# Norm factors by token, a bonus product moved ahead, and a new table of step latencies in a two-layer hybrid decoder kernel

## The chip, the cores and the metric

The kernel runs on one core of one Trainium2 chip. The metric is the device time of one execution in microseconds (us). The core has TensorE (PE; PEld is its weight load), VectorE (DVE), ScalarE (ACT), GpSimd (POOL) and the queues that issue DMAs, SyncE's (SP) among them. Each engine runs its own instructions in the order in which they were emitted and waits on semaphores of the others.

## The reference, cut to what matters

Two layers over 288 tokens (a prompt of 256 and 8 samples of 4) of width 2048, in fp32. Layer 0 mixes by RWKV-7 beside SSD, layer 1 by a gated delta rule (GDN); each layer then has cross attention to a memory and a gated FFN with a short convolution.

```python
for l in range(DEPTH):
    hn = rmsnorm(h, P['norm_mix'][l])
    if l % 2 == 0:
        p_rw, p_ssd = jnp.split(hn @ P['w_in_ab'][i], [RW_PROJ], axis=-1)
        y_rw, sh, s_rw = rwkv7_mix(p_rw, ...)
        y_ssd, cb, s_ssd = ssd_mix(p_ssd, ...)
        mix = jnp.concatenate([y_rw, y_ssd], axis=-1) @ P['w_out_ab'][i]
    else:
        y_c, cb, s_gdn = gdn_mix(hn @ P['w_in_c'][i], ...)
        mix = y_c @ P['w_out_c'][i]
    h = h + mix
    h = h + cross_attn(rmsnorm(h, P['norm_xa'][l]), mem_k[l], mem_v[l], P['w_xq'][l], P['w_xo'][l])
    f, fb = conv_ffn(rmsnorm(h, P['norm_ffn'][l]), st_ffn[l], ...)
    h = h + f
y = rmsnorm(h, P['norm_final'])
```

`rmsnorm` multiplies each token's row by the reciprocal root of its mean square and by a gain. In RWKV each head adds to its output a bonus, the sum over its channels of r·k·rk times v. SSD's sample states follow h = h·decay + state increment. GDN's decay is g = -exp(A)·softplus(a + bias), and its chunks need a triangular solve, as RWKV's do.

## The kernel before, in words

Activations lie with features on the partitions and the 288 tokens along the row. A projection reads fp32 weights from HBM in blocks `raw` of 128x512, which ACT rounds to `wh` and DVE completes by the remainder `wl`; the activations are split likewise into `xH` and `xL`. Each 128x128 block of weights then takes three matmuls of 288 columns into `p_acc` (xH by wh, xL by wh, xH by wl). One such matmul is called a **W** below; there are some 19,900 of them, and in stretches with nothing else they start 0.133 us apart.

The normalization is not applied to the activations but to what a projection gives: `rB` holds each token's factor on all 128 partitions and multiplies `p_acc` when it leaves PSUM (`pad<-p_acc,rB`, `fu<-p_acc,rB`). Squares are summed into `sacc` as the residual `h` is written. `stats_end` then has one matmul of `sacc` with ones, which sums over partitions and spreads the sum over all of them, and a reciprocal root on DVE over 128x288 elements in 12 operations: one for the mean, two for a first guess and three Newton rounds of three (`nx`, `nt`, `rB` in the trace). It is called at six places: at the end of the memory part (for layer 0's mix), ahead of layer 0's cross attention and FFN, ahead of layer 1's mix, cross attention and FFN. The last normalization (`last_norm`) does it by token: three small matmuls a summand put each token's sum on a partition, GpSimd takes the power -1/2, and the factors come back onto all partitions by a diagonal `dg` and a matmul with ones.

In the mixed stages (RWKV with SSD, GDN, cross attention) the weights' matmuls serve as fill between the small steps of the heads. `flow()` is a planner: it holds several streams of jobs, each a generator that yields between steps. The first stream is the fill (projections), the others are prepare, invert, sample, chain and so on. It keeps a clock made of modelled matmul durations; step k of a job of kind `x` may not stand before `LAT[(x, k)]` us after the end of the step ahead of it (1.6 us where the table says nothing, 0 for the fill), and while no step is due it emits fill. What comes out is the order of TensorE's instructions, which is kept as emitted; the other engines are ordered by the tile scheduler.

Names that the steps touch. RWKV (kinds `rwp` prepare, `rwv` invert, `rwt` sample, `rwc` chain, `rwf`) takes 16 heads in 8 pairs: `rkk` is r·k·rk and its matmul with a block of ones `cst` goes to the only `p_row` bank; `AR,h` are the Gram matmuls into `p_ma`, masked into `Gm`; `at_r` and `a8t_r` start the inversion, whose steps are `a_r,a8t_r`, `sx_r,xt_r`, `xc_r,xt_r`, `lo_r,xt_r`, `mx_r,xt_r`, `xc_r,xt_r`, `ac_r,h`, `XTr,yc_r`. `finish` of a pair multiplies by the gate (`SG,gu`) and transposes y (`cst,yr`). SSD (`sdG`, `sdh`, `sd0`, `sdp`) has two groups of 8 sample states: `h<-i_sssd` is loaded, `h,Cx` reads it, `XDs,bs` makes the increment in a PSUM bank, and `hn` is the new state that is stored. GDN (`gdi` inputs, `gdp` prepare, `gdv` invert, `gds` and `gdt` sample, `gdc` chain, `gdf` last finish) takes 16 heads; its decay rows are made once at the start of the stage (`aa`, `sp`, `grows`, `d`), and the last step of its inversion is `X,Atg`, copied by ACT to `yh_g`, then `XTg,yh_g`.

Of the kernel before, what the change touches and what calls it, by code (L numbers as in the profile page):

```python
# [43 lines left out]
def _consts():  # L44
# [50 lines left out]
PV_HALF = POFF["g_mix"][0]  # L95
# [135 lines left out]
def pr(ap):  # L231
    return ap[:, :NP]
# [17 lines left out]
class K:  # L250
# [310 lines left out]
    def last_norm(self, sq):  # L561
# [3 lines left out]
        x = self.mp.tile([128, 3], F32, name="fx")  # L565
# [44 lines left out]
    def conv_silu(self, ps, hist, out_state, wcols, bias, out, out2=None):  # L610
# [170 lines left out]
    def rwkv(self):  # L781
# [53 lines left out]
        def prepare(j, o):  # L835
# [31 lines left out]
            self.stt(ta, ta, 1.0, kk, ADD, MUL)  # L867
            p = self.P("row")
# [36 lines left out]

            Gm = o.Gm = mp.tile([128, 4, 2, 128], F32, name="Gm", tag="Gm", bufs=2)
# [258 lines left out]
    def ssd(self):  # L1165
# [171 lines left out]
        def group(g, os):  # L1337
# [4 lines left out]
            for b in range(B):  # L1342
# [105 lines left out]
    def gdn(self):  # L1448
# [83 lines left out]
        def prepare(h, o):  # L1532
# [27 lines left out]
            for c in range(2):  # L1560
                self.stt(DEC[:, c, :], pb[:, c * 128:(c + 1) * 128], TOK[:, c, 32 + h:33 + h], self.c("negm"), SUB, ADD)
# [563 lines left out]
```

## Time and profile before

| | us |
|---|---|
| median of 3 runs (lowest, highest) | 3385.61 (3383.97, 3388.70) |
| the profiled execution | 3383.89 |
| its span in the trace | 3382.1 |
| memory part, 0 to 107 | 107 |
| layer 0 mix, 107 to 714; out-projection to 790; cross attention to 865 | 758 |
| layer 0 FFN, 865 to 1711 | 846 |
| layer 1 mix, 1711 to 2380; out-projection to 2444; cross attention to 2521 | 810 |
| layer 1 FFN and final norm, 2521 to 3382 | 861 |

The profile is one execution; its time is 1.8 us above the span of its trace and 1.7 us below the median. Stage limits are read off the first and last matmuls of each part, to a few us. TensorE is busy nearly all the time, so what counts is where it waits, and at which clock it runs.

### The profile page before, as it was taken

Reading aid. Unit: us, or ns where it says so; the run is one execution under the profiler, and the core shown is the slowest. Engines: PE = TensorE matmul, PEld = TensorE weight load, DVE = VectorE, ACT = ScalarE, POOL = GpSimd, SP = SyncE. Lnnn points to the kernel's source line nnn. Section 1 sums busy time; section 2 is a strip of 40 time slices with the busy share of each in tenths; the row PEclk is TensorE's granted clock in tenths of the full one; section 3 lists DMA queues with packets and bytes.
Section 4 is the critical chain, followed back from the end, with each engine's and each line's share of the span. In section 5 each row is a group of like instructions: output and inputs, shape, how many; then the busy total and the mean of one; then the engine's idle time right before and its main releaser. Section 6 shows DMA issues by size and latency. Waiting matters only on the chain.

```text
span 3382.1 us, 73169 instructions
## 1 busy us (share of the span) xinstructions
PE 3307.1 (98%) x27952; PEld 3130.2 (93%) x27952; DVE 2392.4 (71%) x5908; ACT 1799.3 (53%) x4435; POOL 86.6 (3%) x267
## 2 busy tenths in 40 slices
PE   9999999899999999999999999999999999999998
PEld 7888778789999999999988888888989999999998
DVE  7777777876766566556688888887776655665665
ACT  7655556545544444444556666666554444443444
POOL 0000000000000000000000000000000000000000
PEclk9999999899999999999999999999999999999999
DMA  8532233576555555555654444445755555555554
GB/s 259 191 99 93 89 101 124 163 235 213 170 165 164 167 163 168 163 165 166 186 154 142 143 147 144 141 145 170 234 181 162 163 166 165 165 166 163 167 165 144
DMA packets 194815, 547.20 MB, mean 162 GB/s; under 512 B 33824, under 2 KB 60064, under 8 KB 194464
## 3 DMA queue, kind: packets, MB, share of 16 engines
q1 hardware_dynamic: 194464, 542.52, 51.5%
q8 instruction: 220, 3.60, 0.4%
q14 instruction: 131, 1.07, 0.1%
HBM read 511.58 MB, written 30.86 MB: 160 GB/s over the span
## 4 chain that ended last, share of the span: by engine, by line
PE 89%; DVE 5%; issue 4%; ACT 1%; DMA 1%; POOL 0%; SPq 0%; DVEq 0%; ACTq 0%; POOLq 0%
PE p_acc L303 73%; PE p_ma L303 5%; PE p_mb L303 4%; PE p_row L303 3%; PE p_y L303 1%; DVE wl L315 1%; PE p_row L311 1%; DMA raw<-i_w_fi 1%; PE p_mb L311 0%; DVE hn L318 0%; ACT wh L328 0%; DVE h L315 0%; PE p_ma L311 0%; DVE cy L318 0%; DMA cache<-i_cv 0%
## 5 line engine op out<-in xcount | busy, mean ns | idle before, releaser
L303 PE MATMUL p_acc<-xH,wh 128*128 128x288 f32 x6464 | 1964.7, 304 | 6.8 <-ACT ost L328 2.9
L303 PE MATMUL p_acc<-xL,wh 128*128 128x288 f32 x6464 | 1912.7, 296 | 4.7 <-DVE xL L315 4.7
L303 PE MATMUL p_acc<-xH,wl 128*128 128x288 f32 x6464 | 1907.4, 295 | 3.8 <-DVE wl L315 3.7
L328 ACT ACTIVATE wh<-raw 128x512 fp32r<-128x512 f32 x1755 | 1100.0, 630 | 1229.7 <-PE p_acc L303 1091.4
L315 DVE TENSOR_TENSOR wl<-raw,wh 128x512 fp32r<-128x512 f32 x1755 | 1203.6, 689 | 621.9 <-ACT wh L328 592.1
L303 PEld LDWEIGHTS p_acc<-xH,wh 128*128 128x128 f32 x6464 | 1214.0, 188 | 36.7 <-issue 13.3
L303 PEld LDWEIGHTS p_acc<-xL,wh 128*128 128x128 f32 x6464 | 1217.1, 188 | 8.3 <-DVE xL L315 5.1
L303 PEld LDWEIGHTS p_acc<-xH,wl 128*128 128x128 f32 x6464 | 1219.0, 189 | 6.0 <-DVE wl L315 5.0
L315 DVE TENSOR_TENSOR pad<-p_acc,rB 128x256 f32<-128x256 f32 x348 | 93.0, 300 | 47.9 <-PE p_acc L303 47.4
L318 DVE SCALAR_TENSOR_TENSOR cy<-pad,pv,cy 128x312 f32<-128x312 f32 x180 | 95.8, 532 | 3.9 <-ACT cy L328 1.7
L318 DVE SCALAR_TENSOR_TENSOR fy<-pad,pv,fy 128x304 f32<-128x304 f32 x176 | 93.8, 533 | 3.1
L315 DVE TENSOR_TENSOR h<-p_acc,h 128x288 f32<-128x288 f32 x128 | 58.4, 456 | 43.6 <-PE p_acc L303 43.1
L592 POOL MEMSET pad<- 128x2 f32 (+2 forms) x174 | 17.5, 102 | 2458.4 <-DVE fy L318 1741.1
L315 DVE TENSOR_TENSOR fu<-p_acc,rB 128x288 f32<-128x288 f32 x88 | 40.2, 457 | 32.2 <-PE p_acc L303 32.2
L328 ACT ACTIVATE sq<-h 128x288 f32<-128x288 f32 x90 | 39.6, 440 | 26.5 <-DVE h L315 26.4
L315 DVE TENSOR_TENSOR sacc<-sacc,sq 128x288 f32<-128x288 f32 x104 | 47.1, 453 | 2.7 <-ACT sq L328 2.6
L315 DVE TENSOR_TENSOR fu<-fu,fy 128x256 f32<-128x256 f32 (+1 forms) x176 | 45.8, 302 | 2.2 <-ACT fy L328 2.2
L328 ACT ACTIVATE osc<-pad 128x3 f32<-128x3 f32 x120 | 22.9, 212 | 40.5 <-DVE pad L315 40.0
L328 ACT ACTIVATE xH<-h,pv 128x288 fp32r<-128x288 f32 x80 | 41.7, 521 | 0.0
L318 DVE SCALAR_TENSOR_TENSOR xL<-h,pv,xH 128x288 fp32r<-128x288 f32 x80 | 41.1, 514 | 0.5 <-ACT xH L328 0.3
L303 PE MATMUL p_acc<-oH,wh 128*128 128x288 f32 x128 | 38.2, 301 | 1.8 <-ACT wh L328 0.8
L315 DVE TENSOR_TENSOR xL<-fu,xH 128x288 fp32r<-128x288 f32 x88 | 39.8, 452 | 0.0
(672 smaller groups left out, 3220.7 us busy)
## 6 DMA issues: line engine op xcount, KB each, us to landing
raw<-i_w_fi SPq DMA_DIRECT2D x352, 512.0 KB, 3.6
raw<-i_w_fo SPq DMA_DIRECT2D x160, 512.0 KB, 3.6
raw<-i_w_c SPq DMA_DIRECT2D x128, 512.0 KB, 3.8
raw<-i_w_ab SPq DMA_DIRECT2D x92, 512.0 KB, 3.8
raw<-i_w_oab SPq DMA_DIRECT2D x32, 512.0 KB, 4.3
raw<-i_w_oc SPq DMA_DIRECT2D x32, 512.0 KB, 3.9
raw<-i_w_xkv SPq DMA_DIRECT2D x31, 512.0 KB, 4.6
raw<-i_w_xq SPq DMA_DIRECT2D x16, 512.0 KB, 4.7
```

Of the source, the lines that this page charges most:

```text
L303: i = self.pe.matmul(out, l, r, start=start, stop=stop)
L311: i = self.pe.transpose(out, a, self.c("ident", r)[:, r])
L315: (eng or self.v).tensor_tensor(out=out, in0=a, in1=b, op=op)
L318: self.v.scalar_tensor_tensor(out=out, in0=a, scalar=sc, in1=b, op0=o0, op1=o1)
L328: self.s.activation(out=out, in_=a, func=f, scale=scale)
L592: self.g.memset(p[:, 0:H], 0.0)
```

## The change

1. `stats_end` uses the by-token way of `last_norm` (now `token_norm`), with the single summand `sacc`; ACT copies the result to `rB`. At six places one large matmul and 12 DVE operations of 128x288 are replaced by three small matmuls, two small DVE operations, a GpSimd power, two DVE operations for `dg`, one large matmul and a copy.
2. RWKV: `rkk` is computed ahead of the first yield of its job, and its matmul and the product with v stand ahead of the Gram matmuls instead of behind them. `finish` yields between `SG,gu` and the transposes of y.
3. SSD: `hn` is made by two operations of 128x512 (decay times state, then plus the PSUM increment) instead of eight of 128x64.
4. GDN's start: the softplus is done with tokens on partitions, on 3x16 columns, and transposed back; SSD's softplus is in that layout already. All heads' decay matrices are made as separate jobs (`gde`) in a tile `DECS`, the factor `ed` goes into `KT_` and `KS` instead of into `u` and `US` (`ud`, `uds` fall away).
5. GDN's heads from 2 on (`EARLY`) take Silu from ACT instead of Tanh and a DVE product, so ACT's tables are loaded 8 times in the program where they were loaded 4 times.
6. `LAT`: `rwv` steps 1 to 8 go from 4.5, 1.6, 2.6, 1.6, ... to 2.7, 0.96, 1.56, 0.96, ...; `sdG` 2 from 0.4 to 2.2; `sdh` 4 from 1.6 to 0.3; `sd0` 0 from 1.6 to 0.96; `xas` 0 from 1 to 3.2; `xat` 4 from 0 to 1.1; `gdt` 6 from 1.6 to 2.1; `gdi` 0 (a fill job) from 0 to 2.4; `gdf` 0 from 1.6 to 5; `gde0` 0 is 18 and `gde` 0 is 1.6. All other entries are the same.
7. The columns of the packed vectors that are halved up front end ahead of `gw`; two small scaled copies `gwh` and `gnh` serve GDN's first two heads.

```diff
     def stats_end(self):
-        ps = self.P()
-        self.mm(ps[:, :N], self.ones, self.sacc)
-        x = self.gt("nx")
-        t = self.gt("nt")
         r = self.big.tile([128, N], F32, name="rB", tag="rB", bufs=2)
-        self.ts(x, ps[:, :N], 1.0 / D, MUL, EPS, ADD)
-        self.rsqrt(r, x, t)
+        self.act(r, self.token_norm([self.sacc]))
         self.rB = r
...
         for i, (r, t) in enumerate(parts):
-            self.mm(p[r, i:i + 1], self.sacc[:, t], self.ones[:, 0:1], stop=False)
-            self.mm(p[r, i:i + 1], sq[:, t], self.ones[:, 0:1], start=False)
+            for n, sq in enumerate(sums):
+                self.mm(p[r, i:i + 1], sq[:, t], self.ones[:, 0:1], start=n == 0, stop=n == len(sums) - 1)
...
             self.stt(ta, ta, 1.0, kk, ADD, MUL)
+            rkk = gt("rkk")
+            self.stt(rkk, r, self.pcol("rk", j), kp, MUL, MUL)
             p = self.P("row")
             yield 2
...
             yield 3
 
+            p = self.P("row")
+            self.mm(p[:, :N], bo64, rkk)
+            self.stt(self.h[:, j, :], p[:, :N], 64.0, v, MUL, MUL)
+
             Gm = o.Gm = mp.tile([128, 4, 2, 128], F32, name="Gm", tag="Gm", bufs=2)
...
-            rkk, BV = gt("rkk"), self.h[:, j, :]
-            self.stt(rkk, r, self.pcol("rk", j), kp, MUL, MUL)
-            p = self.P("row")
-            self.mm(p[:, :N], bo64, rkk)
-            self.stt(BV, p[:, :N], 64.0, v, MUL, MUL)
...
             self.mm(pg[:, :N], o.gu, SG)
+            yield
             p = self.P("mb")
...
                 hn = al("hn", [128, 512], "UV")
-                for h in range(8):
-                    x = slice(64 * h, 64 * h + 64)
-                    self.stt(hn[:, x], h0[:, x], q.CD[:, 8 * g + h, 1 + b:2 + b], ph[:, x], MUL, ADD)
+                self.tt(hn.rearrange("p (h x) -> p h x", x=64), h0.rearrange("p (h x) -> p h x", x=64),
+                        q.CD[:, 8 * g:8 * g + 8, 1 + b:2 + b].to_broadcast([128, 8, 64]), MUL)
+                self.tt(hn, hn, ph, ADD)
                 self.store(d["o_ssds"][b][:, gs], hn)
...
-        self.softplus(x, rg, lambda: gt("sp")[rg])
+
+        p = self.P()
+        self.transpose3(p, rows)
+        xt = mp.tile([128, 3, 48], F32, name="gtt")
...
+        self.softplus(xt[:, :, rg], None, lambda: gt("sp")[:, 0:48].rearrange("p (c x) -> p c x", c=3))
+        p = self.P()
...
         with self.ordered():
-            self.flow(fill, prep, inv, smp, chn)
+            self.flow(fill, dec, prep, inv, smp, chn)
```

How the order changes, at three places. Line numbers of the helpers are one higher in the changed program (L303 is L304, L315 is L316, L318 is L319).

The first place is RWKV's sixth pair of heads. On TensorE the rows of before stand so; between the two `AR,h` there are 12 W, which are left out:

```order
L303 MATMUL p_ma<-AR,h 128x128 x4
L303 MATMUL p_mb<-UV,Gm 64x64 x2
...
L303 MATMUL p_ma<-AR,h 128x128 x4
L303 MATMUL p_row<-rkk,cst 128x288
L303 MATMUL p_mb<-R,XTr 64x64 x2
L303 MATMUL p_acc<-xH,wh 128x288
```

And on DVE, where `rkk` is made in before, behind the masking of the two Gram products:

```order
L315 TENSOR_TENSOR Gm<-p_ma,cst 128x512
L322 TENSOR_SCALAR mu<-mu 32x2
L315 TENSOR_TENSOR Gm<-p_ma,cst 128x512
L315 TENSOR_TENSOR ys<-ys,mu 32x128
L315 TENSOR_TENSOR h<-Gm,rk_5406 64x4x64 x2
L318 SCALAR_TENSOR_TENSOR rkk<-r,pv,kp 128x288
L315 TENSOR_TENSOR at_r<-h,cst 32x128 x4
```

The changed order on TensorE for the same pair, with 12 W between the `rkk` matmul and `UV,Gm` and 12 between the two `AR,h`:

```order
L304 MATMUL p_row<-UVx,BL 128x256
L304 MATMUL p_row<-rkk,cst 128x288
...
L304 MATMUL p_mb<-UV,Gm 64x64 x2
L304 MATMUL p_ma<-AR,h 128x128 x4
...
L304 MATMUL p_mb<-R,XTr 64x64 x2
L304 MATMUL p_ma<-AR,h 128x128 x4
```

The `rkk` matmul has moved from right behind the second Gram product to 12 W ahead of the first; on DVE `rkk` is emitted there with `kp`, ahead of everything that the Gram products feed, and `at_r` no longer stands behind it.

The second place is the norm of layer 1's FFN, on TensorE. Before, the one matmul between W:

```order
L303 MATMUL p_acc<-xH,wl 128x288
L303 MATMUL p_ma<-sacc,ones 128x288
L303 MATMUL p_acc<-xH,wh 128x288
```

And now, with 13 W in all between the last small matmul and `dg,ones` (at the six places in the order of the program 11, 12, 13, 9, 12 and 13):

```order
L304 MATMUL p_acc<-xH,wl 128x288
L304 MATMUL p_ma<-ones,sacc 128x1 x2
L304 MATMUL p_ma<-ones,sacc 32x1
L304 MATMUL p_acc<-xH,wh 128x288
...
L304 MATMUL p_ma<-dg,ones 128x288
L304 MATMUL p_acc<-xL,wh 128x288
```

TensorE has got a second matmul of the chain, which waits for DVE and GpSimd, where it had none.

The third place is the inversion of the same RWKV pair, on TensorE. Before, between `lo_r,xt_r` and `mx_r,xt_r` stand 12 W, and 9 between `mx_r,xt_r` and `xc_r,xt_r`:

```order
L303 MATMUL p_ma<-lo_r,xt_r 32x32 x16
L303 MATMUL p_row<-UVs,Gs 32x64 x2
...
L303 MATMUL p_ma<-mx_r,xt_r 32x64 x16
L303 MATMUL p_mb<-UV,BKT 64x64 x2
L303 MATMUL p_y<-UV,Gm 64x64 x2
...
L303 MATMUL p_ma<-xc_r,xt_r 32x32 x16
```

In the changed order 3 W stand at each of the two, with more of the other streams' small matmuls:

```order
L304 MATMUL p_ma<-lo_r,xt_r 32x32 x16
L312 MATMUL p_row<-cst,v 32x128
L312 MATMUL p_row<-cst,h 64x128 x2
...
L304 MATMUL p_ma<-mx_r,xt_r 32x64 x16
L304 MATMUL p_row<-S0z,ARx 64x64 x8
L304 MATMUL p_mb<-UV,Gm 64x64 x2
...
L304 MATMUL p_ma<-xc_r,xt_r 32x32 x16
```

Over the seven gaps of this pair's inversion the W have gone from 9, 15, 6, 12, 9, 12 and 12 to 3, 9, 6, 3, 3, 6 and 6; the fill that is left over stands elsewhere in the stage. In GDN's heads 2 to 13 the W between `X,Atg` and `XTg,yh_g` have gone from 21 to 3.

## Rows read from the trace of the kernel before

**Rows 1.** The page, section 1: busy time, share of the span, instructions.

```profile
PE 3307.1 (98%) x27952; PEld 3130.2 (93%) x27952; DVE 2392.4 (71%) x5908; ACT 1799.3 (53%) x4435; POOL 86.6 (3%) x267
```

**Rows 2.** Windows by stage: length, busy time of each engine (instructions), clock, DMA.

```profile
107.00:714.00 607.00, 573.69 (x6115) 493.34 (x6116) 473.71 (x1436) 335.32 (x946) 24.27 (x68) 0.98 0.40 126
...
865.00:1711.00 846.00, 845.08 (x6333) 844.31 (x6333) 542.34 (x1018) 392.64 (x781) 5.68 (x50) 1.00 0.55 168
```

**Rows 3.** TensorE's waits, whole span: for whom; us in total, times, longest.

```profile
PE p_row L303 <- DVE rkk L318: 9.1, 3, 3.7
...
PE p_row L303 <- DVE bs L322: 4.4, 5, 1.2
PE p_acc L303 <- DVE wl L315: 3.7, 4, 2.4
PE p_y L303 <- DMA h<-i_sssd: 3.3, 2, 2.9
PE p_acc L303 <- ACT ost L328: 2.9, 2, 2.0
PE p_row L303 <- DVE hn L318: 2.5, 3, 1.1
...
PE p_mb L311 <- DVE S L322: 2.2, 3, 1.0
...
PE p_acc L303 <- ACT osh L328: 1.7, 1, 1.7
```

**Rows 4.** Two windows after long waits; the number behind POOL is the clock.

```profile
637.00:646.00 9.00, 9.00 (x45) 7.93 (x43) 6.22 (x21) 3.60 (x11) 0.00 (x0) 0.50 0.47 146
...
2534.30:2537.70 3.40, 3.40 (x16) 3.40 (x16) 2.23 (x4) 1.74 (x2) 0.10 (x1) 0.50 0.43 149
```

**Rows 5.** Timeline of TensorE, sixth RWKV pair: start, duration, instruction, [idle before, releaser].

```profile
379.25 0.72 PE L303 MATMUL p_row<-rkk,cst 128*128 128x288 f32 x2 [3.69 <-DVE rkk L318]
```

**Rows 6.** Timeline of DVE at the same place.

```profile
376.71 0.67 DVE L315 TENSOR_TENSOR Gm<-p_ma,cst 128x512 f32<-128x512 f32 x1
...
378.61 0.50 DVE L318 SCALAR_TENSOR_TENSOR rkk<-r,pv,kp 128x288 f32<-128x288 f32 x1
```

**Rows 7.** Timeline of DVE, norm of layer 1's FFN: first and last of the 12.

```profile
2521.65 0.45 DVE L324 TENSOR_SCALAR nx<-p_ma 128x288 f32<-128x288 f32 x1
...
2531.87 0.46 DVE L318 SCALAR_TENSOR_TENSOR rB<-nt,rB 128x288 f32<-128x288 f32 x1
```

**Rows 8.** Timeline of the last norm, all engines.

```profile
3369.09 0.20 PE L303 MATMUL p_ma<-ones,sq 128*32 128x1 f32 x2
...
3369.62 0.85 POOL L344 TENSOR_TENSOR fx<-fx,mhalf 128x3 f32<-128x3 f32 x1 [107.59 <-DVE fx L324]
...
3371.14 1.33 PE L303 MATMUL p_ma<-dg,ones 128*128 128x288 f32 x2 [1.85 <-DVE dg L322]
```

**Rows 9.** Timeline of DVE, SSD's first group.

```profile
610.50 1.62 DVE L318 SCALAR_TENSOR_TENSOR hn<-h,cd_s,p_row 128x64 f32<-128x64 f32 x8
```

**Rows 10.** A window in SSD's first group.

```profile
624.00:630.00 6.00, 5.12 (x37) 4.51 (x38) 5.94 (x24) 2.72 (x7) 0.10 (x1) 1.00 0.49 155
```

**Rows 11.** Timeline of an RWKV inversion step: its matmul and its last product.

```profile
389.63 0.45 PE L303 MATMUL p_ma<-a_r,a8t_r 32*32 32x32 f32 x32
...
390.77 0.27 ACT L328 ACTIVATE sx_r<-p_ma 128x128 f32<-128x128 f32 x1
```

**Rows 12.** Timeline of DVE at GDN's start.

```profile
1721.80 1.94 DVE L634 RECIPROCAL sp<-sp 16x288 f32<-16x288 f32 x1
```

**Rows 13.** Timeline of DVE, the same operation in SSD's softplus.

```profile
520.88 0.45 DVE L634 RECIPROCAL sp<-sp 128x48 f32<-128x48 f32 x1
```

**Rows 14.** Timeline of ACT, GDN's last inversion step.

```profile
1789.98 0.27 ACT L328 ACTIVATE yh_g<-p_ma 64x128 f32<-64x128 f32 x1
```

**Rows 15.** Timeline of ACT at a table load.

```profile
1718.07 1.28 ACT L328 ACT_TABLE_LOAD   x1
1719.36 0.20 ACT L328 ACTIVATE na<-pv 16x1 f32<-16x1 f32 x1
```

More of the change, by code (lines that the diff above doesn't have):

```diff
@@ L353, in split, with stack @@
             self.stt(lo, x, gain, hi.bitcast(F32), MUL, SUB)
-    def stack(self, out, x, twin=0, eng=None):
+    def stack(self, out, x, twin=0, eng=None, gain=None):
         hi, lo = out[0:32], out[32 + 32 * twin:64 + 32 * twin]
-        self.act(hi, x)
-        self.act(out[64 - 32 * twin:96 - 32 * twin], x)
-        self.tt(lo, x, hi.bitcast(F32), SUB, eng)
+        self.act(hi, x, scale=1.0 if gain is None else gain)
+        self.act(out[64 - 32 * twin:96 - 32 * twin], x, scale=1.0 if gain is None else gain)
+        if gain is None:
+            self.tt(lo, x, hi.bitcast(F32), SUB, eng)
+        else:
+            self.stt(lo, x, gain, hi.bitcast(F32), MUL, SUB)
     def c(self, name, r=slice(0, 128)):
@@ L1469, in conv @@
             i = 16 * g + h
-            wc = [self.pcol("gw", t * 48 + i) for t in range(4)]
+            if h < EARLY:
+                wc = [gwh[:, (t * 3 + g) * EARLY + h:(t * 3 + g) * EARLY + h + 1] for t in range(4)]
+            else:
+                wc = [self.pcol("gw", t * 48 + i) for t in range(4)]
             ps = yield from project(i)
-            self.conv_silu(ps, hist[:, g, :].rearrange("p (b t) -> p b t", t=3), osc[:, g, :], wc, None, out)
+            self.conv_silu(ps, hist[:, g, :].rearrange("p (b t) -> p b t", t=3), osc[:, g, :], wc, None, out, h >= EARLY)
+        gwh = mp.tile([128, 12 * EARLY], F32, name="gwh")
+        gnh = mp.tile([128, 1], F32, name="gnh")
+        o, n = POFF["gw"]
+        self.ts(gwh.rearrange("p (t g h) -> p t g h", t=4, g=3),
+                self.pv[:, o:o + n].rearrange("p (t g h) -> p t g h", t=4, g=3)[:, :, :, 0:EARLY], 0.5, MUL)
+        self.ts(gnh, self.pcol("gnorm"), 0.5, MUL)
         p = self.proj(("w_ba",), self.hsH, self.hsL, range(KT), M=48)
@@ L1480, in gdn @@
         self.ts(rows[ra], x, 0.5, MUL, 0.5, ADD)
-        x, t = gt("aa")[rg], gt("gg")[rg]
+        x, t = rows[rg], gt("gg")[rg]
         self.tt(x, p[rg, :N], self.rB[rg], MUL)
         self.ts(x, x, self.pcol("gdtb", 0, rg), ADD)
-        self.softplus(x, rg, lambda: gt("sp")[rg])
+        p = self.P()
+        self.transpose3(p, rows)
+        xt = mp.tile([128, 3, 48], F32, name="gtt")
+        self.g.memset(xt, 0.0)
+        self.act(xt[:, 0:2, rg], p[:, 0:256].rearrange("p (c x) -> p c x", c=2)[:, :, rg])
+        self.act(xt[0:32, 2, rg], p[0:32, 256 + 32:256 + 48])
+        self.softplus(xt[:, :, rg], None, lambda: gt("sp")[:, 0:48].rearrange("p (c x) -> p c x", c=3))
+        p = self.P()
+        for c in range(2):
+            self.tr(p[0:48, c * 128:(c + 1) * 128], xt[:, c, :])
+        self.tr(p[0:48, NP:N], xt[0:32, 2, :], slice(0, 32))
         na = mp.tile([48, 1], F32, name="na")
@@ L1526, in inputs, with decays @@
             pz = yield from project(48 + h)
-            z, t = gt("z"), gt("zt")
+            z = gt("z")
             self.tt(z, pz[:, :N], self.rB, MUL)
-            self.act(t, z, AF.Tanh, scale=0.5)
-            self.stt(SZ, t, 1.0, z, ADD, MUL)
+            if h < EARLY:
+                t = gt("zt")
+                self.act(t, z, AF.Tanh, scale=0.5)
+                self.stt(SZ, t, 1.0, z, ADD, MUL)
+            else:
+                self.act(SZ, z, AF.Silu)
+        def decays(h):
+            pb = self.P("ma")
+            self.mm(pb[:, 0:NP], sel[:, h:h + 1].to_broadcast([96, 128]), RG)
+            for c in range(2):
+                self.stt(DECS[:, h, c, :], pb[:, c * 128:(c + 1) * 128], TOK[:, c, 32 + h:33 + h], self.c("negm"),
+                         SUB, ADD)
+            self.act(DECS[:, h], DECS[:, h], AF.Exp)
+            yield
         def prepare(h, o):
```

57 lines of the change are left out of this document (28 added, 29 removed).

## The prediction

> **What bounds the kernel now.** I read the busy times first, then the windows by stage, then TensorE's waits, then the timelines at the waits. TensorE is busy for 3307.1 of 3382.1 us [rows 1], so at most some 75 us of idle time can go, and a slower clock can be avoided; everything else is matmuls that the change leaves alone. The windows say where the idle time is: in layer 0's FFN 6333 matmuls take 846 us, 0.1335 us each, with under 1 us idle, which is the floor for a W [rows 2]; in layer 0's mix 33 of 607 us are idle [rows 2]. The list of waits names what TensorE stood for [rows 3]: `rkk` 9.1 us in three waits, SSD's `bs`, `hn` and the load of `h` 4.4, 2.5 and 3.3, `wl` 3.7, `ost` and `osh` 2.9 and 1.7, `S` 2.2. Each is a few us, but they are nearly all that there is to be had.
>
> A long wait can cost more than itself. After the 2.0 us wait ahead of 2533.5 (the longest of the two for `ost` [rows 3]) TensorE was granted the lower of its clocks, 0.50 or 1.2 GHz: 16 matmuls in 3.40 us [rows 4], where 16 W take 16 × 0.1335 = 2.14. So such a stretch costs 1.3 us. Another follows SSD's first group, at 0.50 for the 9 us shown [rows 4]; by the same share it costs 9 × 1.3 / 3.4 = 3.4. Not every wait does this, so I count the clock only where the trace shows it.
>
> **Part by part.** The sum is made against the profiled execution, 3383.9 us.
>
> *The bonus product.* In the sixth pair TensorE stands 3.69 us for `rkk` [rows 5]. On DVE, `rkk` starts at 378.61 although its inputs are old, because it was emitted behind the masks of the Gram products, the second of which starts at 376.71 [rows 6]. The order after has `rkk` made with `kp` and its matmul 12 W, 1.6 us, ahead of the first `AR,h`; what it then needs is one 0.50 us operation [rows 6] and a free `p_row` bank. The three waits, 9.1, should go, and with the longest a stretch at the lower clock, 1.3, but the planner may put the matmul close behind another user of the single bank: I take -9, between -10.4 and -5. `at_r` also comes 0.5 us earlier on DVE, which pays for the shorter cover of the step behind it.
>
> *The yield in `finish`.* The transposes of y now have W ahead of them where they stood right behind the gate's matmul. This is the wait for `S`, 2.2 [rows 3]: -2.2, between -2.2 and 0, as no step was put behind it that depends on the time.
>
> *The six norms.* The old chain is long but nothing waits for it unless a projection's first block is done: in layer 1's FFN it runs from 2521.65 to 2532.33 on DVE [rows 7], and TensorE's wait for `ost` is what this leaves over. At the end of the memory part and in layer 0's FFN it is the same (`osh` 1.7, the other `ost` 0.9 [rows 3]). These 4.6 us and the 1.3 of clock go. In their place TensorE has a chain of its own. In the last norm it takes 2.05 us from the start of the last small matmul to `dg,ones`, 0.85 of them the power on GpSimd [rows 8]. The new order covers it by 11, 12, 13, 9, 12 and 13 W, 1.47 to 1.74 and once 1.20 us. The shortfalls, 2.05 less these, add up to 12.3 - 70 × 0.1335 = 3.0. A `wl` may get ahead of a step of the chain, 0.7 at half of the sites, +2; the first site also waits for a PSUM bank. Behind `dg,ones` stand the W of the next block, so all of it is lost time. In all -5.9 + 5 = -1, between -5 and +6. DVE is left some 5 us lighter at each site, which hides nothing that TensorE waits for.
>
> *SSD's `hn`.* Eight operations take 1.62 us [rows 9]; two of 128x512 take about 0.68 each, by the mask of the same size out of PSUM [rows 6], and the first does not need the PSUM bank. So bank and `h` come free 0.9 us earlier for each state, although DVE saves only 0.26. DVE is full here, 5.94 of 6 us [rows 10], and a full engine speaks for the small figure: 8 × 0.26 = 2 in the first group. The latency of 2.2 ahead of the next state's read gives the increments more W. Of `bs`, `hn` and `h`, 10.2 us together [rows 3], and the slow clock behind them, 3.4, I take -8, between -13.6 and 0.
>
> *The inversion's latencies.* Steps of RWKV's inversion come closer together: seven gaps with 75 W before and 36 after in the pair shown above. A step needs, from its matmul's end at 390.08 to the end of ACT's product at 391.04, 0.96 us [rows 11]. Gaps of 3 W are 0.4 us of W plus other streams' small matmuls, about as much again. So some steps fall short by a few tenths, others not at all. With 8 pairs and seven gaps, 56 steps, and a third of them short by 0.2 us, it is +4; if half were short by 0.3 it would be +8.4; nothing if the small matmuls cover it. The W so saved stand elsewhere in the stage, where little was waited for.
>
> *GDN's start.* One reciprocal of 16x288 keeps DVE for 1.94 us [rows 12], and a chain of operations on such rows stands among the `wl`, for which TensorE waits 3.7 [rows 3]. With tokens on partitions the reciprocal takes 0.45 [rows 13]. I take -3 for the waits, since transposes there and back are new steps that TensorE can wait for: between -5 and +2.
>
> *GDN's heads.* DVE and ACT lose work, but nothing on TensorE waited for it. What is new is the last inversion step with 3 W, 0.40 us, of cover where it had 21: it needs the copy to `yh_g`, 0.27 [rows 14], plus the passing from engine to engine, which the rows show only as part of the 0.96 above. Twelve heads at 0.1 are +1; at 0.6, if a `wh` gets ahead of the copy, +7; if other waits go instead, -2.
>
> A load of ACT's table takes 1.28 us, and the next activation starts at once behind it [rows 15]. Four more make 5.1 us of ACT, three of them among the heads' steps, one in cross attention. ACT runs its `wh` ahead of TensorE, so I take nothing, with +5 as the upper end if each falls on the path. The Trainium skill (ScalarE: Activation LUTs, What ACT_TABLE_LOAD costs) gives 1.28 us for the load and 1.38 for a drain, 2.66 for a switch; by that the upper end would be +10.6. The row has the load and no gap behind it, so the trace does not show the drain at this place.
>
> *More work on TensorE.* Six norms have three small matmuls more each and GDN's start six transposes more, 24 instructions, at about 0.1 us by the last norm's pace: +2.5, between +1.5 and +3. The halving of fewer vector columns and the other latencies change nothing on TensorE's path; W cover them.
>
> The sum is -9 - 2.2 - 1 - 8 + 4 - 3 + 1 + 2.5 = -15.7. So the execution of the profile would take 3368.2, and the median, 1.7 above it, 3370 us, 0.46% less.
>
> **Rivals.** *More goes than I count* (the whole of SSD's waits and the clock, norms at their better end, inversion covered): -10.4 - 2.2 - 5 - 13.6 + 0 - 5 + 1 + 2.5 = -32.7, 3353 us. For it: the latencies were made for these durations, and fill was plentiful. Against it: DVE is full in SSD.
>
> *The waits move, they don't go*: what is saved by `rkk` and `finish`, 11.2, is given back by short steps (inversion +8.4, norms +4) while SSD's waits follow DVE's load (-2) and GDN gives -3, with +1 and +2.5 as above: -0.3, 3385 us, no change. For it speaks that latencies were cut where no wait was listed before.
>
> *The inversion becomes the bound of layer 0's mix* (slower). Everything else as in my sum, but the closer steps wait: from -15.7 it takes 22.5 us more than the 4 counted to be slower by 0.2%, that is 26.5 / 56 = 0.47 us in each step; at the 0.96 us that a step needs with 0.4 of W and no help from small matmuls, 0.56 each, +31.4 in place of +4, it is +11.7, 3397 us. Against it: in the two gaps shown some ten small matmuls stand beside the 3 W.
>
> **How the numbers follow.** What a measurement of this kernel can tell from no change is about 0.2%, 6.8 us. My forecast, 3370 with a range of its own from 3358 to 3378, gets 0.56; more goes, 0.17; the waits move, 0.18; the inversion binds, 0.09. Faster takes my forecast and the first rival and a little less for the forecast's upper edge: 0.72; same 0.19; slower 0.09. The range from 3349 to 3387 leaves out the slow rival and the far halves of the two others, under 2 in 10.
>
> **What would show it.** Right: no wait for `rkk`, none for `S` in `finish`, no `ost` or `osh` wait at the norms but six waits for `dg` of 0.3 to 1 us; `hn` gone from the list in SSD and no stretch at 0.50 near 640; `wl` waits below 1 us at GDN's start. Wrong: long waits for `dg`; `p_ma` waits for `xt_r` and `sx_r` of half a us each throughout 110 to 570; TensorE waiting for `yh_g` in every GDN head; new stretches at 0.50.

## The result and the profile after

The changed kernel takes 3367.78 us (median of 4 runs, 3367.50 to 3370.56) where the kernel before takes 3384.79 beside it (4 runs): ratio 0.9950, 95% interval 0.9937 to 0.9962. 3370 was forecast, with a range from 3349 to 3387. The profiled execution took 3367.75 us with a span of 3366.0, 16.1 less than that of before. The total came out as the sum had it; several of its terms did not, and they missed in opposite directions.

The page after, section 1, answers to [rows 1]:

```profile
PE 3308.5 (98%) x27994; PEld 3133.4 (93%) x27994; DVE 2331.6 (69%) x5620; ACT 1820.3 (54%) x4505; POOL 91.4 (3%) x280
```

TensorE's waits after, which answer to [rows 3] (for whom; us in total, times, longest):

```profile
PE p_row L304 <- DVE SN L316: 5.5, 3, 2.2
PE p_ma L304 <- DVE dg L323: 4.8, 7, 1.8
PE p_row L304 <- DVE hn L316: 4.4, 4, 1.7
...
PE p_acc L304 <- DVE xL L316: 2.6, 1, 2.6
PE p_row L304 <- DVE XTs L316: 2.3, 1, 2.3
PE p_y L304 <- DMA h<-i_sssd: 1.6, 1, 1.6
...
PE p_ma L304 <- DVE xc_r L316: 1.3, 3, 0.6
PE p_row L304 <- DVE bs L323: 1.2, 2, 0.7
...
PE p_ma L304 <- ACT mx_g L329: 1.0, 1, 1.0
...
PE p_ma L304 <- DVE d L316: 0.6, 1, 0.6
```

`rkk`, `S` in `finish`, `ost`, `osh` and the waits for `wl` are gone. `SN`, `xc_r` and `mx_g` are new, and so are six of the seven waits for `dg` (the last norm had one before). The waits for `hn` grew, from 2.5 to 4.4.

Windows of RWKV, SSD with the out-projection, and GDN's heads (length; busy time of PE, PEld, DVE, ACT, POOL; clock; DMA share; GB/s), first of the kernel before, then of the changed one:

```profile
107.56:608.98 501.42, 485.77 (x5562) 420.76 (x5562) 382.03 (x1131) 290.93 (x829) 21.98 (x63) 0.99 0.36 114
608.98:789.54 180.56, 163.45 (x1118) 147.77 (x1117) 149.56 (x420) 85.73 (x200) 2.30 (x5) 0.95 0.65 204
...
1789.51:2358.37 568.86, 562.72 (x5629) 506.82 (x5628) 464.90 (x1613) 384.15 (x1261) 37.80 (x70) 0.99 0.47 147
```

```profile
107.28:609.43 502.15, 488.57 (x5577) 425.13 (x5577) 380.26 (x1128) 289.76 (x834) 24.72 (x76) 0.99 0.36 114
609.43:785.01 175.58, 164.76 (x1110) 148.25 (x1109) 141.03 (x320) 85.22 (x197) 2.43 (x7) 0.93 0.66 208
...
1780.47:2345.12 564.65, 562.54 (x5658) 507.18 (x5657) 439.01 (x1459) 404.86 (x1322) 36.58 (x70) 1.00 0.47 150
```

Two things hide what such a stretch is worth. The order moves W from one stretch to the next, and the lower clock falls differently in every execution. So below a stretch has two numbers: its time at 0.50, **low**, and its **rest**, the length less 0.1335 us for each W in it and less 0.37 us for each us of low. As W count here the matmuls of weights into `p_acc`, 19,776 in the whole kernel; 288 of the out-projection that go into other banks stay in SSD's rest, in every variant alike. The 0.37 is from runs: 17 executions of the kernel before have mean clocks from 0.988 (3394.42 us) to 0.994 (3377.71 and 3381.38), and a line through all 17 falls by 2.5 us for each 0.001, which is 3385 × 0.001 / 0.5 = 6.8 us of low. The stretch in [rows 4] gives the same, 1.3 us lost in 3.4. The low clock behind the last projection is not counted.

| rest, low (us) | before | after | table alone | code alone (old table) | old inversion latencies | old `hn` |
|---|---|---|---|---|---|---|
| RWKV | 224.2, 6.8 | 221.2, 13.7 | 222.1, 23.9 | 220.7, 23.9 | 222.4, 34.1 | 222.0, 17.1 |
| SSD, out-projection | 89.2, 17.1 | 82.9, 23.9 | 89.3, 20.5 | 87.3, 20.5 | 86.6, 17.1 | 88.0, 27.3 |
| GDN's start | 19.8, 0 | 17.6, 0 | 17.4, 3.4 | 18.4, 0 | 17.6, 0 | 18.5, 0 |
| GDN's heads | 184.3, 6.8 | 178.2, 0 | 180.0, 6.8 | 180.2, 0 | 178.1, 0 | 178.1, 0 |
| all others | 210.7, 6.8 | 210.9, 3.4 | 208.0, 6.8 | 211.5, 3.4 | 209.2, 10.2 | 209.0, 3.4 |
| sum | 728.1, 37.5 | 710.7, 41.0 | 716.8, 61.4 | 718.1, 47.8 | 713.9, 61.4 | 715.6, 47.8 |

The stretches run from the first norm's sums to SSD's first `h,Cx`, to the next norm's sums, then from the fourth norm's sums to the first and to the last `X,Atg`. Two executions of the changed kernel differ by under 1 us in each rest, but in RWKV by 13.7 against 23.9 us of low and in SSD by 23.9 against 13.7.

Over all variants below that leave a stretch itself alone, its rest spreads more: 220.4 to 222.0 in RWKV, 82.9 to 84.9 in SSD, 17.6 to 18.6 at GDN's start (16.0 where the norm ahead of it is the old one), 178.1 to 178.4 in the heads. Differences within these spreads show nothing.

Between the two profiled executions the change is worth 17.4 us at one clock: SSD 6.3, the heads 6.1, RWKV 3.0, GDN's start 2.2. By the runs it is some 15: at a clock of 0.992 a line through 10 executions of the changed kernel stands at 3369.4, the line through 17 of before at 3384.3. The profiled execution of before was one of its faster ones, at a clock of 0.993.

### The profile page after: what moved, and what is told of

It reads as the page before. It is cut to its first block, busy times and chain, and to the rows that moved or that the text cites. A ratio compares the mean times of both kernels' runs of the same rounds, so it can differ in the third digit from the quotient of the medians.

```text
span 3366.0 us, 73087 instructions
## 1 busy us (share of the span) xinstructions
PE 3308.5 (98%) x27994; PEld 3133.4 (93%) x27994; DVE 2331.6 (69%) x5620; ACT 1820.3 (54%) x4505; POOL 91.4 (3%) x280
## 4 chain that ended last, share of the span: by engine, by line
PE 85%; issue 5%; DVE 3%; DMA 1%; ACT 1%; POOL 0%; DVEq 0%; ACTq 0%; POOLq 0%
PE p_acc L304 73%; PE p_ma L304 5%; PE p_mb L304 4%; PE p_row L304 2%; PE p_y L304 1%; PE p_row L312 1%; DMA o_ssds<-hn 1%; DVE wl L316 1%; PE p_mb L312 1%; DMA raw<-i_w_fi 0%; ACT wh L329 0%; PE p_ma L312 0%; DVE hn L316 0%; DVE h L316 0%; DMA cache<-i_cv 0%
## 5 line engine op out<-in xcount | busy, mean ns | idle before, releaser
L304 PE MATMUL p_acc<-xH,wh 128*128 128x288 f32 x6464 | 1965.7, 304 | 2.5 <-ACT xH L329 1.5
L304 PE MATMUL p_acc<-xL,wh 128*128 128x288 f32 x6464 | 1913.5, 296 | 2.7 <-DVE xL L316 2.6
L304 PE MATMUL p_acc<-xH,wl 128*128 128x288 f32 x6464 | 1906.6, 295 | 0.0
L316 DVE TENSOR_TENSOR wl<-raw,wh 128x512 fp32r<-128x512 f32 x1755 | 1203.9, 689 | 627.5 <-ACT wh L329 599.6
L304 PEld LDWEIGHTS p_acc<-xH,wh 128*128 128x128 f32 x6464 | 1214.0, 188 | 33.9 <-issue 10.3
L304 PEld LDWEIGHTS p_acc<-xL,wh 128*128 128x128 f32 x6464 | 1216.3, 188 | 7.0 <-DVE xL L316 3.4
L304 PEld LDWEIGHTS p_acc<-xH,wl 128*128 128x128 f32 x6464 | 1218.7, 189 | 1.3
L316 DVE TENSOR_TENSOR pad<-p_acc,rB 128x256 f32<-128x256 f32 x348 | 91.6, 299 | 45.5 <-PE p_acc L304 44.8
L319 DVE SCALAR_TENSOR_TENSOR cy<-pad,pv,cy 128x312 f32<-128x312 f32 x162 | 86.4, 533 | 14.4 <-ACT cy L329 10.3
L319 DVE SCALAR_TENSOR_TENSOR fy<-pad,pv,fy 128x304 f32<-128x304 f32 x176 | 93.7, 533 | 3.1
L316 DVE TENSOR_TENSOR h<-p_acc,h 128x288 f32<-128x288 f32 x128 | 58.4, 456 | 43.7 <-PE p_acc L304 43.3
L591 POOL MEMSET pad<- 128x2 f32 (+2 forms) x174 | 17.1, 100 | 2107.8 <-DVE fy L319 1451.8
L316 DVE TENSOR_TENSOR fu<-p_acc,rB 128x288 f32<-128x288 f32 x88 | 40.2, 457 | 32.3 <-PE p_acc L304 32.3
L316 DVE TENSOR_TENSOR sacc<-sacc,sq 128x288 f32<-128x288 f32 x104 | 47.3, 455 | 3.2 <-ACT sq L329 3.1
L316 DVE TENSOR_TENSOR fu<-fu,fy 128x256 f32<-128x256 f32 (+1 forms) x176 | 45.8, 303 | 0.0
L319 DVE SCALAR_TENSOR_TENSOR xL<-h,pv,xH 128x288 fp32r<-128x288 f32 x80 | 41.2, 515 | 0.5 <-ACT xH L329 0.3
L329 ACT ACTIVATE UX<-US,cst 96x128 fp32r<-96x128 f32 x128 | 39.2, 388 | 1.7 <-DVE US L316 0.8
L316 DVE TENSOR_TENSOR xL<-fu,xH 128x288 fp32r<-128x288 f32 x88 | 39.7, 452 | 0.0
L304 PE MATMUL p_acc<-oH,wh 128*128 128x288 f32 x128 | 38.0, 299 | 1.5 <-ACT oH L329 0.7
```

Source lines behind the costliest of these rows:

```text
L304: i = self.pe.matmul(out, l, r, start=start, stop=stop)
L316: (eng or self.v).tensor_tensor(out=out, in0=a, in1=b, op=op)
L319: self.v.scalar_tensor_tensor(out=out, in0=a, scalar=sc, in1=b, op0=o0, op1=o1)
L329: self.s.activation(out=out, in_=a, func=f, scale=scale)
L591: self.g.memset(p[:, 0:H], 0.0)
```

## The experiments

Ratios are to the kernel before, run beside each; 0.9950 [0.9937, 0.9962] is the changed kernel's.

**The bonus product put back.** The `rkk` product and matmul return behind the Gram products:

```diff
-            rkk = gt("rkk")
-            self.stt(rkk, r, self.pcol("rk", j), kp, MUL, MUL)
...
+            rkk, BV = gt("rkk"), self.h[:, j, :]
+            self.stt(rkk, r, self.pcol("rk", j), kp, MUL, MUL)
+            p = self.P("row")
+            self.mm(p[:, :N], bo64, rkk)
...
```

> The changed kernel with the bonus product alone put back behind the Gram products (same latency table). Layer 0's mix up to the next norm's sums takes 677.7 us in the changed kernel and 682.0 before. Theory (the move swapped one wait for another): the waits for SN ahead of the rkk matmul (2.2, 2.2 and 1.2 us) go, waits of 2.5 to 3.7 for rkk come back in two or three pairs, and the mix takes 676 to 681, the kernel 3366 to 3371. Rival (the move is worth the 9 to 10 us of the forecast, and something else in the stage lost them): the mix takes 686 or more, the kernel 3376 or more.

Ratio 0.9961 [0.9949, 0.9974], 3372.38 us. The mix takes 683.1 us; both numbers lie between the theory's ranges and the rival's. RWKV's rest is 222.9 in place of 221.2, SSD's 86.5 in place of 82.9. TensorE's waits in this kernel's RWKV stretch:

```profile
PE p_row L304 <- DVE rkk L319: 2.9, 2, 1.7
PE p_row L304 <- DVE XTs L316: 2.5, 1, 2.5
...
PE p_row L304 <- DVE SN L316: 1.2, 2, 0.9
```

The waits swap, as the theory said, though `rkk` comes back with only 2.9, at most 1.7 at a time; `SN` falls from 5.5 to 1.2. In its own stretch the move gains nothing clear: TensorE idles there for 11.7 us without it and 13.6 with it, and 1.7 us of rest are about the spread. The sum of rests is 4.4 us more without the move, 3.6 of them in SSD, where the planner's order has 928 W in place of 916 and the waits for `hn` are 6.9 us in place of 4.4. How the move reaches SSD was not tried.

**The old norm.** `stats_end` as before:

```diff
...
-        self.act(r, self.token_norm([self.sacc]))
+        self.ts(x, ps[:, :N], 1.0 / D, MUL, EPS, ADD)
+        self.rsqrt(r, x, t)
```

> The changed kernel with the norm factors alone by the old way (one matmul of sacc and 12 operations on DVE). Theory (a norm's price is what TensorE waits at its own place): the six waits for dg, 3.0 us together, and 18 small matmuls, about 2, go; the wait for ost of 2.0 with its stretch at the lower clock comes back in layer 1's FFN and those for osh and ost of 1.7 and 0.9 elsewhere. The FFN of layer 1 takes 846 in place of 843.8, the kernel 3366 to 3371. Rival (a lighter DVE behind each norm is what helps, in the mixed stages above all): 3373 or more, with more idle time behind the first and fourth norm.

Ratio 0.9938 [0.9926, 0.9951], 3363.74 us, below the theory's range, and the interval overlaps the changed kernel's. In layer 1's FFN the wait for `ost` is 1.3 us and brings no low clock; that stretch takes 844.0, not 846. The sum of rests is 709.2 against 710.7; GDN's start, right behind such a norm, has 16.0 in place of 17.6, SSD 84.9 in place of 82.9. The norm by token gains nothing and may cost some us.

**The old `hn`.** Eight operations a state:

```diff
...
-                self.tt(hn, hn, ph, ADD)
+                for h in range(8):
+                    x = slice(64 * h, 64 * h + 64)
+                    self.stt(hn[:, x], h0[:, x], q.CD[:, 8 * g + h, 1 + b:2 + b], ph[:, x], MUL, ADD)
```

> The changed kernel with SSD's new states alone made by eight operations of 128x64 again. Theory (shorter hold of the PSUM bank and of h is what took SSD's waits from 17.1 to 10.8 us): from SSD's first read of h to the next norm's sums it takes 178.5 to 181 in place of 175.6, the kernel 3370.5 to 3374. Rival (the latencies of sdG and sdh did it): within 1 us of 175.6, the kernel 3366.5 to 3369.

Ratio 0.9972 [0.9963, 0.9981], 3375.19 us. From SSD's first read to the next norm it takes 181.95 us; both are a little above the theory's ranges. The rest is 88.0 against 82.9. Waits of this stretch:

```profile
PE p_row L304 <- DVE hn L319: 3.9, 3, 2.0
PE p_row L304 <- DVE bs L323: 2.8, 2, 1.6
PE p_y L304 <- DMA h<-i_sssd: 2.7, 2, 1.8
...
PE p_row L312 <- DVE yss L316: 2.3, 1, 2.3
PE p_ma L304 <- DVE bs L323: 1.1, 1, 1.1
```

`bs` is back with 3.9 us in all, against 1.2. The theory holds: 5 us are the two wide operations', with the spread 3 to 5.

**The old table.** Every old entry is back, the new kinds `gde0` and `gde` are kept; of its entries these, among others:

```diff
-("rwv", 1): 2.7, ("rwv", 2): 0.96, ("rwv", 3): 1.56, ("sdG", 2): 2.2, ("sdh", 4): 0.3, ("gdi", 0): 2.4
+("rwv", 1): 4.5, ("rwv", 3): 2.6, ("sdG", 2): 0.4, ("sdh", 4): 1.6
...
```

> The changed kernel with every entry of the latency table as before, but for the two kinds that are new with the decay jobs. Theory (the code parts carry the gain, the table hardly any): layer 0's mix 675 to 680 (RWKV's inversion steps are apart again, minus some 3; SSD plus 0 to 3), GDN with its out-projection 723 to 727 in place of 723.6, the kernel 3363 to 3371. Rival (the table carries most of it): layer 0's mix 682 or more and GDN 730 or more, the kernel 3377 or more.

Ratio 0.9979 [0.9970, 0.9988]. The mix takes 684.2 us, as the rival had it, GDN with its out-projection 724.3, as the theory had it, and the kernel 3378.06, the rival's. So with the new code the table is worth about half of the change: 10 of 17 us by the medians, 7.4 of 17.4 by the rests.

**No Silu.** `EARLY = 2` becomes `EARLY = 16`.

> The changed kernel with all 16 GDN heads by Tanh and a DVE product, so without Silu and without the four table loads that go with it. The heads' stretch (first to last X,Atg less 0.1335 us for each W in it) takes 178.2 us in the changed kernel, 186.8 before and 180.2 with the old latencies. Theory (a lighter DVE and ACT in each head is what gave some 6.6 us there): 181 to 184, the kernel 3371 to 3374. Rival (it is the factor ed folded into KT and KS and the decays made ahead, Silu gives nothing): 177 to 179, and the 1.0 us wait for mx_g, which stands where the tables are loaded, goes; the kernel 3366 to 3368.

Ratio 0.9956 [0.9941, 0.9971], 3374.58 us, just above the theory's range, with a clock of 0.992. The heads take 181.4 by the measure of the expectation, 180.1 of rest with 3.4 of low, against 178.2: Silu is worth some 2 us, the lower part of what the theory gave it. The wait for `mx_g` is gone.

**The old softplus.** GDN's start on rows of 16x288:

```diff
...
-        self.softplus(xt[:, :, rg], None, lambda: gt("sp")[:, 0:48].rearrange("p (c x) -> p c x", c=3))
+        self.softplus(x, rg, lambda: gt("sp")[rg])
...
```

> The changed kernel with GDN's softplus alone back on rows of 16x288. GDN's start (from the norm's sums to the first X,Atg, less 0.1335 us for each W) takes 17.6 us in the changed kernel and 19.8 before. Theory (the long operations on DVE among the wl are what TensorE waited for): waits for wl and for d of 3 to 5 us come back, six transposes go, 19.5 to 21.5, the kernel 3369.5 to 3372. Rival (the start gained by its new order and by the Gram-like decay product moved into jobs of its own): 17 to 18.5, the kernel 3367 to 3369.

Ratio 0.9950 [0.9936, 0.9964], 3370.46 us. The waits in GDN's start:

```profile
PE p_acc L304 <- DVE wl L316: 1.9, 1, 1.9
PE p_ma L304 <- DVE d L316: 1.4, 1, 1.4
PE p_ma L304 <- DVE sel L316: 1.4, 1, 1.4
```

In the changed kernel `wl` is not waited for there and `d` for 0.6. The start less its W takes 22.3 us, above the theory's range; 2.5 of that are 6.8 us of low, and the rest is 19.8 in place of 17.6. Variants that leave the start alone have up to 18.6, so 1 to 2 us are shown, at the place that the theory named; in the whole kernel they can't be told from the spread.

**Another bank for `rkk`.** `P("row")` becomes `P("mb")`.

> The changed kernel with the rkk product in a bank of mb (two banks, shared with the chain) in place of the only row bank. Theory (what rkk now waits for is the row bank, held until DVE has made SN from it): the waits for SN of 2.2, 2.2 and 1.2 us and two stretches at the lower clock go, the RWKV stretch (first norm to SSD's first read, less its W) takes 220 to 223 in place of 226.2, the kernel 3362 to 3365. Rival (the chain needs its two banks, the wait comes back there): 225 to 228, the kernel 3366 to 3370.

Ratio 0.9941 [0.9926, 0.9956], 3367.70 us. The RWKV stretch less its W takes 227.7 us, both as the rival had them; its rest is 224.0, more than 221.2. Its longest waits:

```profile
PE p_mb L304 <- DVE S L323: 4.9, 3, 2.4
PE p_row L304 <- DVE XTs L316: 2.9, 1, 2.9
```

The 5.5 us for `SN` have become 1.2 and the chain's banks have 4.9 in their place, as the rival said.

**The old inversion latencies.** Only the eight entries of `rwv` are put back.

> The changed kernel with the eight latencies of RWKV's inversion alone as before. Theory of the forecast (closer steps cost some 4 us of new short waits): waits for xc_r, sx_r and a_r go, the RWKV stretch less its W takes 221 to 224 in place of 226.2, the kernel 3362 to 3366. Rival (the old table as a whole made that stretch 3.3 us longer; closer steps make room): 227 to 230, the kernel 3368 to 3372.

Ratio 0.9965 [0.9953, 0.9977]. The forecast's theory falls. `xc_r`, `sx_r` and `a_r` are no longer waited for, but the stretch less its W takes 235.0 us and the kernel 3376.63, above the rival's ranges too. Of the 8.8 us more in RWKV 7.5 are low, 34.1 us in place of 13.7, and its rest of 222.4 is about the spread; SSD's rest rises to 86.6. The windows of RWKV and SSD in this kernel:

```profile
106.12:623.51 517.39, 501.21 (x5624) 438.88 (x5624) 383.35 (x1139) 293.77 (x844) 25.98 (x77) 0.97 0.35 113
623.51:793.89 170.38, 153.86 (x1061) 138.33 (x1060) 137.87 (x309) 81.08 (x187) 2.33 (x6) 0.95 0.65 209
```

RWKV has 47 instructions more on TensorE than in the changed kernel, SSD 49 fewer: steps that are further apart take 48 W out of SSD's stretch, where TensorE now idles for 170.38 - 153.86 = 16.5 us in place of 10.8.

**The changed kernel again.**

> The changed kernel once more, unchanged, so that the two variants of this call stand beside it on one chip, and to see how far one execution differs from another. Ratio to before 0.994 to 0.9955. If the spread of single executions is the clock (the granted clock of a run against its time), then 0.001 of mean clock goes with 2.5 to 3 us; if it is anything else, times at one clock spread as widely as all.

Ratio 0.9945 [0.9931, 0.9958], 3366.61 us; the clock theory holds for the spread (0.992 and 3371.23, 0.994 and 3363.61), to 1 or 2 us: two runs at 0.993 took 3366.60 and 3370.76. The median clock of its six runs is 0.993, that of the 17 runs of before 0.990.

**The table alone.** The kernel before with the new `LAT`.

> The kernel before with the new latency table alone (the decay jobs, which it lacks, have no use for their entries). Theory (the table pays only with the shorter steps of the changed code; with the old long steps on DVE its closer steps fall short): no gain, 3383 to 3395, ratio 0.999 to 1.003, more waits in RWKV and SSD. Rival (the table gives its 7 to 10 us by itself, by leaving more fill for SSD): 3373 to 3379, ratio 0.996 to 0.998.

Ratio 0.9979 [0.9970, 0.9988], 3379.90 us: the rival's ratio, but not its reason, for SSD gains nothing (928 W in place of 925, rest 89.3 in place of 89.2). GDN's heads lose 4.3 us of rest, GDN's start 2.4, RWKV 2.1; its clock is 0.9905, that of before beside it 0.990.

**`rkk` between the Gram products.**

```diff
                 p = self.P("ma")
                 yield
+                if q == 1:
+                    pb = self.P("row")
+                    self.mm(pb[:, :N], bo64, rkk)
+                    self.stt(self.h[:, j, :], pb[:, :N], 64.0, v, MUL, MUL)
```

> The changed kernel with the rkk product between the two Gram products: its matmul stands 9 to 12 W further on, right ahead of the second. Theory (the row bank is free by then, DVE having made SN): the waits for SN of 2.2, 2.2 and 1.2 us go and none for rkk comes, and less their W and their time at the lower clock the RWKV stretch takes 216 to 219 in place of 220.7; the kernel 2 to 6 us below the unchanged one. Rival (the wait is not worth more than the fill that it displaces, as with the bank of mb): the same within 2 us.

Ratio 0.9945 [0.9933, 0.9958]. Of the 5.5 us for `SN` 1.2 stay; waits for `h` are new:

```profile
PE p_row L304 <- DVE XTs L316: 2.9, 1, 2.9
PE p_ma L304 <- DVE h L316: 1.6, 3, 0.6
PE p_ma L304 <- DVE xc_r L316: 1.5, 3, 0.7
PE p_row L304 <- DVE SN L316: 1.2, 2, 0.9
```

The product's matmul waits at no pair, but RWKV's rest is 221.0 against 221.2 and 220.4 in the changed kernel's two executions, SSD's is 85.3, and the kernel takes 3368.23: nothing gained, the rival.

**That and the old norm together.**

> The rkk product between the Gram products, and the norm factors by the old way, all else as changed. Theory (both gains add up): 3 to 10 us below the unchanged changed kernel, ratio to before 0.991 to 0.9935. Rival (the two are within the spread of the clock): the same within 2 us.

Ratio 0.9945 [0.9931, 0.9959], 3367.22 us; sum of rests 711.1 against 710.7. The rival again: no version tried here has an interval clear of the changed kernel's on the fast side.

## Why the prediction was right, point by point

*The bound and the total.* The limit was TensorE's small waits, and the sum of -15.7 stands beside -16.1 in the profiled executions. That they agree so closely is luck. For RWKV and SSD the bonus, the yield, `hn` and the inversion had -15.2; less their W the two stretches fell by 0.5 and 3.8. For the heads the sum had +1; they fell by 8.6. The two errors cancel. Of the terms, four were mis-sized: the bonus, `hn`, the inversion and the heads. Of the signs named, those for `rkk`, `S`, `ost`, `osh` and `wl` came, and six waits for `dg` of 0.3 to 0.8 us. `hn` did not leave the list, and the stretch at 0.50 near 640 stayed, at 633. New stretches at 0.50, a sign of being wrong, came too: RWKV and SSD have four each where they had two.

*The bonus product, -9.* The step that failed is "a free `p_row` bank". The order shown ahead of the prediction has `UVx,BL` right ahead of the `rkk` matmul, both in the single bank, and DVE empties it only by `SN`, which stands there behind 14 small operations, those that make `AR` and `h` among them. TensorE and DVE after, in the sixth pair:

```profile
371.45 0.38 PE L304 MATMUL p_row<-UVx,BL 64*128 64x256 f32 x1
374.00 1.33 PE L304 MATMUL p_row<-rkk,cst 128*128 128x288 f32 x2 [2.17 <-DVE SN L316]
```

```profile
373.26 0.69 DVE L316 TENSOR_TENSOR SN<-p_row,S0z 128x512 f32<-128x512 f32 x1
```

[rows 5] has 3.69 us at that place. Of the 9.1 us for `rkk` 4.3 came back ahead of the same matmul, as waits for `SN`, and 1.2 for `SN` ahead of another matmul into the bank. Another wait into the same bank grew, for `XTs`, to 2.3 us. Before it was:

```profile
PE p_row L303 <- DVE XTs L315: 0.5, 1, 0.5
```

The term of -9 is mis-sized: by undoing the move it is 4.4 us of rest, and none of it clear in RWKV. The two other places tried for the product remove 4.3 of the 5.5 and gain nothing.

*The yield, -2.2.* The waits for `S` in `finish` are gone.

*The norms, -1.* The shortfall was 3.0 by the count of W; the seven waits for `dg` are 4.8 us, of which the last norm's is 1.8, so 3.0. No `wl` added its 2 us. The wait for `ost` went with its low clock, and layer 1's FFN takes 843.8 in place of 846.2. The small loss elsewhere, which the experiment with the old norm suggests, leaves the term near nothing or above it.

*SSD, -8.* The rest fell by 6.3, and undoing `hn` alone costs 5.1. TensorE's idle time fell from 17.1 to 10.8 us: `bs` lost 4.7 (with 1.5 in a second bank before), `h` 1.7, and 1.5 went from a wait that the prediction did not list, for the out-projection's `xL`; `hn` took 1.9 more. Before:

```profile
PE p_acc L303 <- DVE xL L315: 4.1, 1, 4.1
```

The part that failed is the 3.4 of clock: low in that stretch was 17.1 us before, 23.9 and 13.7 in two executions after, so it did not go. That DVE was full did not decide it.

*The inversion, +4.* The short waits are there (`xc_r` 1.3, `a_r` 0.7, `sx_r` 0.2 in the list for this stretch), some 2 of the 4 us. What failed is the sentence that the W so saved stand "where little was waited for": with the new code 48 of them stand in SSD's stretch, where TensorE idled, and undoing the eight latencies costs 3.7 us of rest there and a lower clock in RWKV. The term as measured by undoing it is a gain: 3.2 us in the sum of rests, and 9 to 10 in the medians, of which by 0.002 of clock some 5 are the clock. The intervals of the ratios still touch, 0.9965 against 0.9950 and 0.9945.

*GDN's start, -3.* It was -2.2, with a spread of 1.

*GDN's heads, +1.* It was -6.1, and 6.8 us less of low. The step "nothing on TensorE waited for it" failed. Waits of the heads' stretch before, and then after:

```profile
PE p_row L303 <- PE p_ma L303: 1.9, 6, 0.3
PE p_row L311 <- DVE S L318: 1.0, 1, 1.0
PE p_acc L303 <- ACT xH L328: 0.9, 1, 0.9
PE p_ma L303 <- ACT junk L1546: 0.9, 1, 0.9
PE p_row L303 <- DVE S L318: 0.9, 1, 0.9
```

```profile
PE p_ma L304 <- ACT mx_g L329: 1.0, 1, 1.0
PE p_acc L304 <- ACT xH L329: 0.9, 1, 0.9
```

The idle time in this stretch fell from 6.1 us to 2.1 (568.86 - 562.72 before, 564.65 - 562.54 after); the other 2.1 us of the rest stand in TensorE's busy time and are not explained. The 6.8 us of low need not be the change: they followed the wait of 0.9 us for `xH`, which both kernels have, and in the changed one none follow it. By the experiments the table alone takes the rest to 180.0 and the code alone to 180.2, so most of it comes by either way; Silu has 1.9 of it. Which of the other parts has what was not tried. No wait for `yh_g` came up in the list.

*The table loads, nothing.* One of them shows, ACT's and TensorE's rows after:

```profile
1806.09 1.28 ACT L329 ACT_TABLE_LOAD   x1
1807.38 0.54 ACT L329 ACTIVATE KQ<-cy 128x256 f32<-128x256 f32 x2
1807.83 0.20 ACT L329 ACTIVATE mx_g<-p_ma 128x64 f32<-128x64 f32 x1
```

```profile
1808.09 0.42 PE L304 MATMUL p_ma<-mx_g,xt_g 32*32 32x64 f32 x16 [0.96 <-ACT mx_g L329]
```

The load of 1.28 us stands ahead of the copy that TensorE waits 0.96 us for, so the loads cost about 1 us here where the term was nothing; without Silu and its loads the heads still take 1.9 more. The next activation starts 0.01 us behind the load; the 1.38 us drain that the Trainium skill gives (ScalarE: Activation LUTs, What ACT_TABLE_LOAD costs) is not seen here either.

*More work on TensorE, +2.5.* No run measures this term by itself; it is in the rests above.

*The clock.* The prediction counted it where one trace had it. That was the weak place of the method. The median clocks of the runs are 0.990 and 0.991 for before (three sets of runs), 0.991 for the code alone and for the old inversion latencies, 0.9905 for the table alone, 0.993 for the changed kernel run again, and 0.992 to 0.994 for the others, which have the new table and all parts of the code but one or two. By 2.5 us for 0.001, some 5 to 7 us of the medians' difference of 17 to 22 are the clock. Why it rises only with table and code together was not settled.

## What to carry to other kernels

When a matmul is moved in an order, ask of its PSUM bank what is written there just ahead and which engine has to empty it; a single bank that changes hands back to back can cost what its emptier has queued, here 2.17 us behind 14 small operations. In a planner's table, look at where the fill goes that a cut latency saves, and for the stretch that has none left; here one experiment shows it, with the new code, and with the old code SSD gained nothing. Judge a stretch only after taking out the work that moved through its ends and its time at the lower clock: two executions of one program differed more by the clock than most parts of this change are worth.

## What the runs showed of the hardware

One program's executions spread over 17 us (3377.71 to 3394.42) with mean clocks from 0.994 to 0.988, though TensorE is busy for 98% of the time; and in these traces the length of a wait alone does not decide it. In the changed kernel, TensorE goes to the lower clock at 633 behind a wait of 0.74 us, in SSD (a row of its timeline, and a window behind it):

```profile
632.57 1.56 PE L304 MATMUL p_row<-Xs,Ls 32*32 32x64 f32 x16 [0.74 <-DVE hn L316]
```

```profile
633.00:643.00 10.00, 10.00 (x45) 8.34 (x43) 7.11 (x20) 4.80 (x15) 0.00 (x0) 0.50 0.37 125
```

In the kernel before, the 1.7 us for `osh` [rows 3], at 117, were followed by none until 175. In the changed kernel's second execution RWKV has 23.9 us of low where the first has 13.7, with nearly the same waits.

GpSimd's power on 128x3 took 0.85 us at three of the seven norms, the last among them [rows 8], and 1.17 to 1.23 us at the four others, where a `wl` runs on DVE beside it for some 0.5 us (row of the tile `fx`: minimum, median, maximum in ns; then one of the four on the timeline):

```profile
L345 POOL TENSOR_TENSOR fx<-fx,mhalf x7: 849/1167/1232, 108.5 to 3353.5; 128x3 f32<-128x3 f32 x7
```

```profile
862.19 0.67 DVE L316 TENSOR_TENSOR wl<-raw,wh 128x512 fp32r<-128x512 f32 x1
...
862.34 1.23 POOL L345 TENSOR_TENSOR fx<-fx,mhalf 128x3 f32<-128x3 f32 x1 [74.11 <-DVE fx L325]
```

The Trainium skill (GPSIMD Engine Reference, Key points) says that GpSimd shares its SBUF interfaces with VectorE and contends with operations that have two SBUF inputs, as `wl` has; it gives no size, and the rows here agree, with up to 0.38 us.
